# Seven small moves of work and waits in a two-layer trunk kernel: empty steps, earlier transposes, new homes, and 16 writes on another queue

## The chip, the core and the metric

The kernel runs on one core of a Trainium2 chip. The metric is the device time of one execution in microseconds. A core has five engines with queues of their own, each of which runs its instructions in order: TensorE (PE, matrix products into PSUM), VectorE (DVE), ScalarE (ACT), GpSimd (POOL) and SyncE (SP, which here issues nearly all DMAs). [...] PE's clock is granted by a throttle; 1.00 is full speed.

## The reference

One sequence of 1024 tokens, width 1024, float32, two layers. The core of it, with norms left out:

```python
for layer in range(2):
    hn = rms_norm(h, ...)
    if layer == 0:                     # "even": gated MLP + gated delta rule
        a_uv, b_qkv, b_z, b_beta, b_a = split(hn @ w_in_e)
        a_out = gmlp_spatial_gate(gelu(a_uv), ...)      # 128-token chunks, 4 groups
        b_out = gated_deltanet(b_qkv, b_z, ...)         # 64-token chunks, 4 heads, unit lower-triangular solves
        h = h + concat([a_out, b_out]) @ w_out_e
    else:                              # "odd": differential attention, 8 heads x 2 maps, alibi, causal
        o = diff_attention(hn @ w_qkv_o, ...)
        h = h + o @ w_out_o
    h = h + square(relu(rms_norm(h) @ w_mlp1[layer])) @ w_mlp2[layer]      # width 4096
    h = h + (p[layer] @ w_ple_proj[layer]) * sigmoid(rms_norm(h) @ w_ple_gate[layer])
```

## The kernel before, in words

**Tiles.** The residual h lies in DRAM (`h_dram`) as eight feature tiles of 128 features by 1024 tokens; in SBUF it is held as two halves of 512 tokens (`h` or `hf` = 0, 1), so a tile is 128x512. Nearly every product of full width is done with three float32r matmuls: each operand is split into a rounded part `hi` (an ACT cast, line 221) and a remainder `lo` (a DVE subtraction, line 222), and `mm3` (line 204) multiplies hi·hi, hi·lo and lo·hi. A call of `mm3` is called a unit below. Weights come through a ring of eight `raw` buffers (`RB = 8`), `TB = 4` scratch tiles are shared through `tmp()`, and PSUM has two buffers for each of the tags mm, tr, aux and sc.

**The order.** The program is traced in Python and then ordered by a planner, which issues, on each engine, what its own time model finds ready, by priority (the order of writing; `high_priority` raises it). `Ordered.behind` adds an order of issue without a semaphore. `pe.floor` puts the next PE instructions behind a given one.

**Layer 0, `even_mix` (line 1281).** The projections are a generator `fill`; `pump(n)` advances it. The delta rule's serial chain is cut into steps, and `chunk` (nested in `even_mix`) issues, for each entry of its list `parts`, the steps that the letters name ("s" the state's recurrence, "i" the inverse, "p" the preparation) and then a share of units of `fill`. First `solve` (line 1670) solves the 32x32 diagonal blocks on DVE and stores them to `solved`; then `inverse(c)` (line 1714) loads them back (`inv<-solved`), transposes them on DVE (line 1728), and merges blocks to 128 by products `py`, `pz` on PE with copies between them; the last copy (line 1764) completes `xt`, which `step(c)` reads in its product `pvn`. For the first chunk the call is

```python
chunk(none, invs[0], f0, FILLC, ("p", "i", "i", "i", "i", "ip"), bound=True)
```

with `FILLC = 48` units over six entries; `bound=True` sets a floor, so that a step comes behind the units already issued. The eight chunks that follow hide their chain under the other projections, and `mix_out` (line 1229) closes the stage.

**Layer 1, `attention` (line 893).** A loop over 64 blocks (8 heads x 8 query blocks of 128) calls `pump()` four times per block. Each call advances the q/k/v projections by the table `MARKS` (call number, units done), and, past call `TAIL`, one step of `tails()`: `put_halves` (line 1113) reads stored attention outputs back from `o_dram` into a ring of four, `put_o` (line 1103) transposes one on PE (tag tr) and splits it on ACT and DVE into the buffers that held the normed h; `mix_part` (line 1205) then multiplies the first 6 (half 0) or 5 (half 1) heads by `w_out`, adds the residual row tile from DRAM (line 1225) and stores it. After the loop `mix_out` does the remaining heads, 2 for half 0 and 3 for half 1; between its steps the two functions in `close` are called: the last block's value product, and `put_o(7, 1)`, which needs that block's output scaled by POOL (line 1099). At its end, for half 0, it computes the rms of h (matmuls with ones, a POOL power at line 258, matmuls that spread the rows, an ACT copy to `rb`, line 265) and splits the normed h for the MLP (lines 1268 to 1273).

**MLP and PLE.** `mlp` (line 275) is a seven-product (Strassen-Winograd) scheme. In layer 1 its output tiles are also stored token by token: `turn` (line 516) transposes 32x32 blocks on DVE and issues four DMAs of 64 KB to `by_token`. `ple_out` (line 634) is again a seven-product scheme; `raw` (line 651) loads weight blocks into the `raw` ring, `rows` (line 700) reads residual rows from `by_token`, `close` gates and stores the output.

Of the kernel before, what the change touches and what calls it, by code (L numbers as in the profile page):

```python
# [11 lines left out]
F32 = mybir.dt.float32  # L12
# [6 lines left out]
P = 128  # L19
# [12 lines left out]
KA = (6, 5)  # L32
MARKS = ((64, 50), (192, 144), (223, 168))
TAIL = 220
FILLA, FILLB, FILLC = 36, 60, 48
# [79 lines left out]
class Trunk:  # L115
# [132 lines left out]
    def rms(self, half, sqs, ms=None, rows=True):  # L248

        nc = self.nc  # L250
        if ms is None:
            pt = self.aux_ps()
            for t in range(4):
                self.pe.matmul(pt[:, t : t + 1], lhsT=sqs[:, t * P : (t + 1) * P], rhs=self.ones[:, 0:1], start=True, stop=True)
            ms = self.sp.tile([P, 4], F32, tag="ms", name=self.nm("ms"))
            nc.vector.tensor_scalar(ms, pt[:, 0:4], 1.0 / D, EPS, ALU.mult, ALU.add)  # L256
        r = self.sp.tile([P, 4], F32, tag=f"r{half}", name=self.nm("r"))
        nc.gpsimd.tensor_tensor(r, ms, self.mhalf[:, 0:4], ALU.pow)  # L258
        rb = None
        if rows:  # L260
            pb = self.aux_ps()
            for t in range(4):
                self.pe.matmul(pb[:, t * P : (t + 1) * P], lhsT=r[:, t : t + 1].to_broadcast([P, P]), rhs=self.ident, start=True, stop=True)
            rb = self.sp.tile([P, HT], F32, tag=f"rb{half}", name=self.nm("rb"), bufs=1)
            nc.scalar.copy(rb, pb)
        return r, rb

    def mlp(self, x, x_tags, gain, w1, w2, gain_next, h_dram, p, last):
# [239 lines left out]

        def turn(m, h):

            t = self.tmp()
            nc.vector.transpose(t, acc[m][h])
            for i in range(4):  # L520
                f0 = (m % 4) * P + 32 * i
                nc.sync.dma_start(by_token[h][m // 4].rearrange("(a c) f -> c a f", c=32)[:, :, f0 : f0 + 32], t[32 * i : 32 * i + 32].rearrange("c (a r) -> c a r", r=32))

# [110 lines left out]
    def ple_out(self, pT, acc, by_token, gain, wg, wpj, out):  # L634
# [258 lines left out]
    def attention(self, w_qkv, w_out, gain_next, h_dram):  # L893
# [3 lines left out]
        hs, r = list(self.hs), list(self.r)  # L897
        self.mixed = [[None] * KT, [None] * KT]

        al = self.slot("B", [P, S], F32, "al")  # L900
# [212 lines left out]
        def put_halves():  # L1113
# [42 lines left out]
        def tails():  # L1156
            puts = put_halves()
            for hf in range(2):
                while state[1] < 160 + 8 * hf:
# [9 lines left out]
        for g in range(8 * NB + 2):  # L1169
# [35 lines left out]
    def mix_part(self, h, n, w_out, h_dram):  # L1205
# [3 lines left out]
        def load(m):  # L1209
            if m < KT:  # L1210
                res = self.tmp()
                nc.sync.dma_start(res, h_dram[m, :, cols])
                return res

        ahead = load(0)
        for m in range(KT):
            if m % 2 == 0:
                w = self.weight(w_out[0 : n * P, m * P : (m + 2) * P], n, 256, nc.gpsimd)
            res, ahead = ahead, load(m + 1)
# [5 lines left out]
            nc.vector.tensor_tensor(res, res, ps, ALU.add)  # L1225
            nc.sync.dma_start(h_dram[m, :, cols], res)


    def mix_out(self, h, acc, w_out, h_dram, gain_next, k0=0, late=0):

# [5 lines left out]
        for m in range(KT):  # L1236
# [5 lines left out]
            ps = begun.pop() if begun else self.mm_ps()  # L1242
            if late and m == 0:
                begun.append(self.mm_ps())
                for q, k in itertools.product(range(2), range(late, n)):
                    self.mm3((ps, begun[0])[q], w.at(k, slice(q * P, (q + 1) * P)), self.mixed[h][k0 + k], k == late, False)
                    yield
            for i in range(n - late if late and m < 2 else 0, n):
                k = (i + late) % n
# [4 lines left out]
                self.pe.floor = None  # L1254
                if i < n - 1:
                    yield
# [5 lines left out]
        if h == 0:  # L1262
            self.rb[0] = self.rms(0, self.sqs[0])[1]
            self.rb_mark = self.pe.mark
            lows = []
            for m in range(KT):
                a = acc(m)
                inst = nc.vector.scalar_tensor_tensor(a, a, gain_next[:, m : m + 1], self.rb[0], ALU.mult, ALU.mult)
                if m > 1:
                    self.pe.behind(inst, lows[m - 2])  # L1270
                hi, lo = self.hs_new[0][m] = self.hs_parts(0, m)
                nc.scalar.copy(hi, a)  # L1272
                lows.append(nc.vector.tensor_tensor(lo, a, f32(hi), ALU.subtract).ins.name)  # L1273
        yield
# [6 lines left out]
    def even_mix(self, first, rows_of_rest, rest_of_x, w_in, ws, bs, conv, a_log, dt_bias, v_gain, o_gain, masks, w_out, gain_next, h_dram):  # L1281
# [432 lines left out]
        def inverse(c):  # L1714
# [47 lines left out]
            for h in range(G):  # L1762
                self.pe.matmul(pz[:, h], lhsT=x64[:, h], rhs=yt[:, h], start=True, stop=True)
            (nc.vector.tensor_copy if c < NC - 1 else nc.scalar.copy)(xt[0:64, :, 64:P], pz)
            ch[c] = xt
# [56 lines left out]
        def mixing():  # L1822
# [9 lines left out]
            side = second_gates()  # L1832
            yield from beside(self.mix_out(0, acc, w_out, h_dram, gain_next, late=G), side, 4, 8)
            for _ in side:
# [111 lines left out]
def trunk(tc, x, p, ln_mix_e, w_in_e, gmlp_v_gain, gmlp_ws, gmlp_bs, gdn_conv, gdn_a_log, gdn_dt_bias, gdn_out_gain,  # L1946
          w_out_e, ln_mix_o, w_qkv_o, attn_q_gain, attn_k_gain, diff_lambda, attn_sub_gain, w_out_o, ln_mlp, w_mlp1,
          w_mlp2, ln_ple, w_ple_gate, w_ple_proj, masks, out):
    with ExitStack() as ctx:
# [54 lines left out]
        for layer in range(2):  # L2004
# [68 lines left out]
```

## Time and profile before

| | us |
|---|---|
| median of 3 runs | 2499.24 |
| lowest, highest | 2496.97, 2501.38 |
| the profiled execution's own time | 2502.64 |
| its span (first to last instruction) | 2500.9 |
| PE busy | 2471.4 (99%) |
| DVE / ACT / POOL busy | 1866.2 / 1289.2 / 303.9 |

The mean granted clock of PE is 0.996. A row of waits reads "engine, tile, line that waited <- what ended the wait: total, times, longest". A row of a timeline reads "start, duration, engine, line, operation, out<-in, shape, count", and in brackets the idle time before it with what ended it. `SPq` rows are DMA issues in SP's queue. In rows of stretches, each engine's busy time is followed by its count of instructions, then come the granted clock, DMA share and GB/s.

### The profile page before, as it was taken

Reading aid. Unit: us, or ns where it says so; the run is one execution under the profiler, and the core shown is the slowest. Engines: PE = TensorE matmul, PEld = TensorE weight load, DVE = VectorE, ACT = ScalarE, POOL = GpSimd, SP = SyncE. Lnnn points to the kernel's source line nnn. Section 1 sums busy time; section 2 is a strip of 40 time slices with the busy share of each in tenths; the row PEclk is TensorE's granted clock in tenths of the full one; section 3 lists DMA queues with packets and bytes.
Section 4 is the critical chain, followed back from the end, with each engine's and each line's share of the span. In section 5 each row is a group of like instructions: output and inputs, shape, how many; then the busy total and the mean of one; then the engine's idle time right before and its main releaser. Section 6 shows DMA issues by size and latency. Waiting matters only on the chain.

```text
span 2500.9 us, 39804 instructions
## 1 busy us (share of the span) xinstructions
PE 2471.4 (99%) x13567; PEld 2108.1 (84%) x13567; DVE 1866.2 (75%) x3642; ACT 1289.2 (52%) x2585; POOL 303.9 (12%) x272
## 2 busy tenths in 40 slices
PE   9999999999999999999999999999999999999999
PEld 7898897888888887888899999987788888887877
DVE  7787776597667879566568888886886677788677
ACT  6543443465455435454366766664655455445443
POOL 0211231000000000000244443431000000000000
PEclk9999999999999999999999999999999999999999
DMA  8384645457556856553347776799375558657773
GB/s 253 114 248 115 171 142 178 140 161 246 169 182 224 264 180 191 187 173 111 119 100 167 163 173 153 174 252 287 125 235 191 173 187 283 213 180 202 237 215 110
DMA packets 567924, 461.96 MB, mean 185 GB/s; under 512 B 256676, under 2 KB 429736, under 8 KB 567720
## 3 DMA queue, kind: packets, MB, share of 16 engines
q1 hardware_dynamic: 533912, 455.21, 60.3%
q10 hardware_dynamic: 33808, 4.20, 1.1%
q8 instruction: 107, 1.75, 0.3%
q14 instruction: 97, 0.79, 0.1%
HBM read 322.95 MB, written 136.33 MB: 184 GB/s over the span
## 4 chain that ended last, share of the span: by engine, by line
PE 89%; DVE 4%; DMA 4%; issue 1%; ACT 1%; SPq 1%; POOL 0%; ACTq 0%; DVEq 0%; POOLq 0%
PE mm L76 78%; PE po L76 3%; PE qk L76 2%; PE aux L76 2%; PE tr L79 1%; DMA raw<-in_w_ple_gate_dram 1%; DMA raw<-in_w_mlp_dram 1%; DVE w L222 1%; DMA spill<-early 0%; DMA a_dram<-lg 0%; DMA guv<-uv_dram 0%; DVE acc L282 0%; DMA aT<-a_dram 0%; DVE g L222 0%; PE pvn L76 0%
## 5 line engine op out<-in xcount | busy, mean ns | idle before, releaser
L76 PE MATMUL mm<-g,w 128*128 128x512 f32 x2592 | 604.0, 395 | 1.5 <-DVE g L222 1.1
L221 ACT CAST w<-raw 128x512 fp32r<-128x512 f32 x598 | 365.0, 616 | 449.6 <-PE mm L76 364.7
L76 PEld LDWEIGHTS mm<-g,w 128*128 128x128 f32 x2592 | 486.7, 188 | 116.5 <-DVE g L222 2.0
L76 PE MATMUL mm<-hi,w 128*128 128x512 f32 x1728 | 555.2, 398 | 0.3 <-ACT hi L1272 0.3
L76 PE MATMUL mm<-w,hi 128*128 128x256 f32 (+2 forms) x2528 | 504.9, 295 | 0.8 <-ACT t L1500 0.6
L222 DVE TENSOR_TENSOR w<-raw,w 128x512 fp32r<-128x512 f32 (+1 forms) x510 | 349.6, 692 | 167.9 <-ACT w L221 160.4
L76 PEld LDWEIGHTS mm<-w,hi 128*128 128x128 f32 x2528 | 402.8, 189 | 16.0 <-ACT t L1500 0.8
L76 PEld LDWEIGHTS mm<-hi,w 128*128 128x128 f32 x1728 | 325.4, 189 | 74.3 <-ACT hi L1272 0.7
L76 PE MATMUL mm<-w,lo 128*128 128x256 f32 (+2 forms) x1264 | 368.5, 292 | 0.0
L76 PE MATMUL mm<-lo,w 128*128 128x512 f32 x864 | 341.6, 395 | 1.0 <-DVE lo L1273 1.0
L76 PE MATMUL mm<-t,w 128*128 128x512 f32 x1152 | 270.7, 394 | 1.2 <-ACT w L221 1.2
L76 PEld LDWEIGHTS mm<-t,w 128*128 128x128 f32 x1152 | 216.5, 188 | 52.2 <-ACT w L221 1.6
L76 PEld LDWEIGHTS mm<-w,lo 128*128 128x128 f32 x1264 | 238.2, 189 | 5.8
L76 PEld LDWEIGHTS mm<-lo,w 128*128 128x128 f32 x864 | 163.4, 189 | 38.0 <-DVE lo L1273 1.4
L222 DVE TENSOR_TENSOR g<-graw,g 128x512 fp32r<-128x512 f32 x216 | 147.5, 687 | 11.2 <-DMA gd<-g 6.8
L221 ACT CAST g<-graw 128x512 fp32r<-128x512 f32 x216 | 132.6, 617 | 43.9 <-DMA graw<-gd 16.4
L1048 ACT ACTIVATE lg<-lg,nm 128x128 f32<-128x128 f32 (+7 forms) x128 | 99.2, 776 | 77.0 <-DVE nm L1045 76.2
L258 POOL TENSOR_TENSOR r<-ms,mhalf 128x4 f32<-128x4 f32 x12 | 13.2, 1103 | 1006.7 <-DVE ms L256 981.2
L222 POOL TENSOR_TENSOR w<-raw,w 128x512 fp32r<-128x512 f32 (+1 forms) x88 | 115.4, 1330 | 142.3 <-ACT w L221 85.0
L348 ACT ACTIVATE g<-g 128x512 f32<-128x512 f32 x96 | 60.5, 631 | 119.3 <-DVE g L282 112.4
L1045 DVE CUSTOM_DVE_ANT_0 lg<-qk,al 128x512 f32<-128x512 f32 (+3 forms) x128 | 74.7, 587 | 27.2 <-PE qk L76 22.0
L76 PE MATMUL mm<-ohi,w 128*128 128x512 f32 x256 | 87.1, 405 | 0.7 <-DVE t L1225 0.7
(332 smaller groups left out, 3522.0 us busy)
## 6 DMA issues: line engine op xcount, KB each, us to landing
raw<-in_w_mlp_dram SPq DMA_DIRECT2D x352, 256.0 KB, 3.4
graw<-gd SPq DMA_DIRECT2D x224, 256.0 KB, 2.8
gd<-g SPq DMA_DIRECT2D x192, 256.0 KB, 3.0
raw<-in_w_ple_gate_dram SPq DMA_DIRECT2D x76, 256.0 KB, 3.6
acc<-h_dram SPq DMA_DIRECT2D x64, 256.0 KB, 4.3
keep<-in_w_mlp_dram SPq DMA_DIRECT2D x64, 256.0 KB, 4.5
raw<-in_w_in_e_dram SPq DMA_DIRECT2D x60, 256.0 KB, 3.7
h_dram<-acc SPq DMA_DIRECT2D x48, 256.0 KB, 2.7
```

The source lines that it names most:

```text
L76: self._next(self.engine.matmul(*a, **k))
L79: self._next(self.engine.transpose(*a, **k))
L221: self.nc.scalar.copy(hi, src)
L222: (lo_engine or self.nc.vector).tensor_tensor(lo, src, f32(hi), ALU.subtract)
L258: nc.gpsimd.tensor_tensor(r, ms, self.mhalf[:, 0:4], ALU.pow)
L348: nc.scalar.activation(g, src, AF.Relu)
L1045: nc.vector.tensor_tensor_reduce(out=lg[:, k0:k1], in0=ps[:, : k1 - k0], in1=al[:, u0 + k0 : u0 + k1], scale=-1.0, scalar=3.0e38 if c == 0 ...
L1048: nc.scalar.activation(lg[:, :n], lg[:, :n], AF.Exp, bias=nm[:, r, nch - 1 : nch], scale=-1.0, accum_out=me.sums[:, b, r : r + 1])
```

## The change

- **First inverse.** Three empty entries stand between "p" and the first "i"; the 48 units are shared over nine entries and not six.
- **Last copy of an inverse.** For chunks 4 to 6 ACT does it and not DVE (chunk 7 had ACT already).
- **Tail of the attention.** `TAIL` 220 becomes 205 and the last mark moves from call 223 to 227; `put_halves` issues its first four loads when `tails` starts; `begin` of the last head comes one block earlier.
- **`mix_part`.** Residual rows get homes of their own (slots c0, c1 and sqs0 in turn, and no longer a `tmp`), are loaded two tiles ahead, and a tile is closed (added, stored) after the second unit of the next tile.
- **`mix_out` in layer 1.** `put_o(7, 1)` is called after step 16 of half 0 and not after step 12; half 1 begins with heads 5 and 6 of its first two tiles; the rms sums of half 0 are issued at tile 2 of half 1 and its rows at tile 4, where before both came at the end of half 0, held ahead of tile 6.
- **`turn`.** The 16 writes of the last four tiles are issued from GpSimd's queue and no longer from SP's.
- **`ple_out`.** The first four residual rows go to tiles lo10 to lo13 and no longer to four of the eight `raw` buffers.

```diff
-MARKS = ((64, 50), (192, 144), (223, 168))
-TAIL = 220
+MARKS = ((64, 50), (192, 144), (227, 168))
+TAIL = 205
...
-        def turn(m, h):
+        def turn(m, h, queue=nc.sync):
...
-                turn(q, 1)
+                turn(q, 1, nc.gpsimd)
...
-        rows(0, 0, [self.raw(1, HT)[:, 0] for _ in R])
+        rows(0, 0, [self.hp.tile([P, HT], F32, tag=f"lo1{q}", name=self.nm("rows")) for q in R])
...
             for n in range(4):
                 load(n)
+            yield
...
-                if b == 6 + (hd == 6) and hd < 7:
+                if b == 6 and hd < 7:
                     begin(hd + 1)
...
+                i = next(self.res_home)
+                res = self.slot(f"c{i}", [P, HT], F32, "res") if i < 2 else self.sp.tile([P, HT], F32, tag="sqs0", name=self.nm("res"), bufs=1)
...
+        def close():
+            m, ps = open_.pop(0)
+            res = ahead.pop(0)
+            self.pe.behind(nc.vector.tensor_tensor(res, res, ps, ALU.add), self.pe.mark)
+            nc.sync.dma_start(h_dram[m, :, cols], res)
+            load(m + 2)
...
+                if m and k == 1:
+                    close()
...
-                if h == 1 and k0 and (m, i) == (6, 0):
-
-                    self.pe.floor = self.rb_mark
+            if h == 1 and k0 and m in (2, 4):
+                self.pe.floor = self.pe.mark
+                self.later.pop(0)()
+                self.pe.floor = None
...
+            def sums():
+                self.r[0] = self.rms(0, sqs, rows=False)[0]
+
+            def rows():
+                self.rb[0] = self.rows(0, self.r[0])
+                lows = []
+                for m in range(KT):
...
+            self.later = [sums, rows]
+            if not k0:
+                sums()
+                rows()
...
-            (nc.vector.tensor_copy if c < NC - 1 else nc.scalar.copy)(xt[0:64, :, 64:P], pz)
+            (nc.vector.tensor_copy if c < G else nc.scalar.copy)(xt[0:64, :, 64:P], pz)
...
-        chunk(none, invs[0], f0, FILLC, ("p", "i", "i", "i", "i", "ip"), bound=True)
+        chunk(none, invs[0], f0, FILLC, ("p", "", "", "", "i", "i", "i", "i", "ip"), bound=True)
...
-                    if n + 1 in (4 * (KT - KA[0]), 6 * (KT - KA[0])):
+                    if n + 1 in (4 * (KT - KA[0]), 8 * (KT - KA[0])):
                         close.pop(0)()
-            for _ in T.mix_out(1, lambda m: acc_of(m, 1), (w_out_e, w_out_o)[layer][0], h_dram, gain[3 * layer + 1], KA[1] * layer):
+            for _ in T.mix_out(1, lambda m: acc_of(m, 1), (w_out_e, w_out_o)[layer][0], h_dram, gain[3 * layer + 1], KA[1] * layer, first=(0, 1) if layer else ()):
```

More of the change, by code (lines that the diff above doesn't have):

```diff
@@ L258, in rms, with rows @@
         nc.gpsimd.tensor_tensor(r, ms, self.mhalf[:, 0:4], ALU.pow)
[L259 to L266, printed above, removed]
+        return r, self.rows(half, r) if rows else None
+    def rows(self, half, r):
+        pb = self.aux_ps()
+        for t in range(4):
+            self.pe.matmul(pb[:, t * P : (t + 1) * P], lhsT=r[:, t : t + 1].to_broadcast([P, P]), rhs=self.ident, start=True, stop=True)
+        rb = self.sp.tile([P, HT], F32, tag=f"rb{half}", name=self.nm("rb"), bufs=1)
+        self.nc.scalar.copy(rb, pb)
+        return rb
     def mlp(self, x, x_tags, gain, w1, w2, gain_next, h_dram, p, last):
@@ L1157, in tails @@
             puts = put_halves()
+            next(puts)
             for hf in range(2):
@@ L1222, in mix_part, with mix_out @@
                 self.mm3(ps, w.at(k, slice((m % 2) * P, (m % 2 + 1) * P)), self.mixed[h][k], k == 0, k == n - 1)
+                if m and k == 1:
+                    close()
                 if k % 2:
                     yield
-            nc.vector.tensor_tensor(res, res, ps, ALU.add)
-            nc.sync.dma_start(h_dram[m, :, cols], res)
-    def mix_out(self, h, acc, w_out, h_dram, gain_next, k0=0, late=0):
+            open_.append((m, ps))
+        close()
+    def mix_out(self, h, acc, w_out, h_dram, gain_next, k0=0, first=()):
         nc = self.nc
@@ L1832, in mixing @@
             side = second_gates()
-            yield from beside(self.mix_out(0, acc, w_out, h_dram, gain_next, late=G), side, 4, 8)
+            yield from beside(self.mix_out(0, acc, w_out, h_dram, gain_next, first=range(G, KT)), side, 4, 8)
             for _ in side:
```

42 lines of the change are left out of this document (20 added, 22 removed).

## The prediction

> **What bounds the kernel now.** First the page, for the engine that is always busy, then what PE waits for.
>
> ```profile
> span 2500.9 us, 39804 instructions
> PE 2471.4 (99%) x13567; PEld 2108.1 (84%) x13567; DVE 1866.2 (75%) x3642; ACT 1289.2 (52%) x2585; POOL 303.9 (12%) x272
> ```
>
> PE sets the time. No edit takes a matmul away, so all that can be won is the 2500.9 - 2471.4 = 29.5 us in which PE is idle, and whatever the idle time costs afterwards. The view of PE's waits lists it nearly whole:
>
> ```profile
> engine line waited for: us in total, times, longest us
> PE py L76 <- issue: 4.4, 1, 4.4
> PE aux L76 <- DVE ms L256: 3.3, 1, 3.3
> PE pvn L76 <- DVE xt L1764: 2.5, 1, 2.5
> PE tr L79 <- POOL o L1099: 2.1, 1, 2.1
> PE tr L79 <- DVE ss L938: 1.6, 1, 1.6
> ...
> PE mm L76 <- DVE lo L1273: 1.0, 1, 1.0
> ...
> PE mm L76 <- DVE t L1225: 0.7, 1, 0.7
> ```
>
> Single waits, each at one place; that makes the question seven small questions. The four longest have an aftermath, which the view of stretches shows where the granted clock (after POOL's figure) falls:
>
> ```profile
> core 0: us, PE busy (x) PEld busy (x) DVE busy (x) ACT busy (x) POOL busy (x), PEclk, DMA share, GB/s
> 207.32:212.11 4.79, 4.79 (x26) 3.86 (x27) 2.21 (x6) 0.53 (x3) 0.00 (x0) 0.50 0.35 55
> 382.78:386.19 3.41, 3.41 (x14) 2.92 (x13) 1.18 (x5) 0.41 (x1) 0.33 (x1) 0.50 0.88 266
> 1737.87:1741.28 3.41, 3.41 (x11) 2.83 (x10) 1.49 (x3) 1.78 (x3) 0.00 (x0) 0.50 0.20 77
> 2417.12:2420.53 3.41, 3.41 (x10) 2.63 (x9) 2.53 (x5) 0.74 (x2) 0.46 (x1) 0.50 0.68 199
> ```
>
> PE is busy there, but at half speed, so half of each stretch is lost: 2.4 us after the first wait, 1.7 us after each of the other three. A wait of 2.1 us costs 3.8 us. [...]
>
> **The change part by part.**
>
> *A. Empty entries before the first inverse.* The timelines of SP, DVE and PE in turn:
>
> ```profile
> 198.91 0.34 SPq L1685 DMA_DIRECT2D solved<-work  x1
> 202.56 0.33 SPq L1723 DMA_DIRECT2D inv<-solved  x1
> 206.91 0.31 DVE L1728 STREAM_TRANSPOSE inv<-inv 128x128 f32<-128x128 f32 x1 [0.63 <-DMA inv<-solved]
> 201.16 0.63 PE L76 MATMUL mm<-hi,w 128*128 128x512 f32 x2
> 201.86 0.63 PE L76 MATMUL mm<-hi,w 128*128 128x512 f32 x2
> 207.32 0.64 PE L76 MATMUL py<-inv,am 32*32 32x32 f32 x16 [4.38 <-issue]
> ```
>
> The product py stands in PE's order after two entries of 8 units, but its operand makes a round trip through DRAM (store at 198.91, load from 202.56, transpose at 206.91). With nine entries (5, 5, 6, 5, 5, 6, 5, 5, 6) py comes after 26 units and not 16. A unit takes 201.86 - 201.16 = 0.70 us, so PE has 10 x 0.70 = 7.0 us more to do before it, against 4.38 us of waiting: 2.6 us of cover is left. Saved: 4.38 + 2.4 = 6.8 us (ends 0 and 6.8). Late next: the inverse's steps now lie 5 to 6 units (3.5 to 4.2 us) apart and not 5.6; what lies between two of them on DVE and ACT is a few copies, and the LAG of three slots gives 10 us of room. No instruction is added. I book 1 us for a step that comes late.
>
> *B. The last copy on ACT for chunks 4 to 6.* Timeline of DVE, then ACT:
>
> ```profile
> 378.25 2.18 DVE L1544 SCALAR_TENSOR_TENSOR guv<-guv,rv,vg 128x128 f32<-128x128 f32 x8
> 380.34 0.69 DVE L222 TENSOR_TENSOR w<-raw,w 128x512 fp32r<-128x512 f32 x1
> 380.94 0.41 DVE L1764 COPY xt<-pz 64x256 f32<-64x256 f32 x1
> 378.98 0.59 ACT L1580 CAST ahi<-pab 128x512 fp32r<-128x512 f32 x1 [1.26 <-PE pab L79]
> ```
>
> Chunk 6's copy queues on DVE behind nine instructions of other work, while ACT had been idle 1.26 us before 378.98. On ACT it can run at about 378, before PE reaches pvn. Saved: 2.5 + 1.7 = 4.2 us (0 to 4.2). For chunks 4 and 5, where PE did not wait, ACT takes on 0.4 us; it is 52% busy, so nothing is booked.
>
> *C. `put_o(7, 1)` four units later.*
>
> ```profile
> 1736.58 1.04 POOL L1099 TENSOR_TENSOR o<-o,of 128x512 f32<-128x512 f32 x1
> 1737.67 0.97 PE L79 MATMUL tr<-ident,o 128*128 128x128 f32 x4 [2.07 <-POOL o L1099]
> ```
>
> PE stood from 1735.60 until POOL was done. Four units are 2.8 us, over 2.07. The transposes' split, needed by head 7's products, is then covered by the four units of heads 5 and 6 that half 1 now begins with. No DMA moves. Saved: 2.07 + 1.7 = 3.8 us (0 to 3.8).
>
> *D. Sums at tile 2, rows at tile 4.* In the groups of the stretch 1753.8 to 1770 and on the page:
>
> ```profile
> L1268 DVE SCALAR_TENSOR_TENSOR acc<-acc,cols,rb 128x512 f32<-128x512 f32 x8 | 5.9, 747 | 0.8 <-ACT rb L265 0.8
> ...
> L258 POOL TENSOR_TENSOR r<-ms,mhalf 128x4 f32<-128x4 f32 x12 | 13.2, 1103 | 1006.7 <-DVE ms L256 981.2
> ```
>
> Before, the rows are held only ahead of tile 6 of 8; now they start at tile 4, two tiles of three units earlier, 4.2 us, against the 1.0 us that the MLP's first `lo` is late. Between sums and rows lie the same 4.2 us for a POOL power of 1.1 us. Saved 1.0 us (bounds -1 to 1.0: a row product that comes too early holds PE's queue).
>
> *E. `ple_out`: four `raw` buffers freed, 16 writes off SP.* Timelines of SP and DVE, then the view of `by_token`:
>
> ```profile
> 2408.04 2.56 SPq L522 DMA_DIRECT2D by_token<-t  x4
> 2410.70 7.34 SPq L653 DMA_DIRECT2D raw<-in_w_ple_gate_dram  x6
> 2415.73 0.69 DVE L643 TENSOR_TENSOR raw<-raw,raw 128x512 f32<-128x512 f32 x1 [2.92 <-DMA raw<-in_w_ple_gate_dram]
> 2416.34 0.15 DVE L256 TENSOR_SCALAR ms<-aux 128x4 f32<-128x4 f32 x1
> 2416.57 1.01 POOL L258 TENSOR_TENSOR r<-ms,mhalf 128x4 f32<-128x4 f32 x1 [67.58 <-DVE ms L256]
> 2418.20 0.17 DVE L734 TENSOR_SCALAR rh<-r 128x4 f32<-128x4 f32 x1
> ...
> L522 SPq DMA_DIRECT2D by_token<-t x16: 326/488/1062, 2395.2 to 2410.1; - x16
> ```
>
> The 3.3 us at ms is not ms's own: ms stands in DVE's queue behind a subtraction that waits 2.92 us for a weight block. Those loads wait in SP's queue behind the writes (16 x 0.49 = 7.8 us of issue) and for a free `raw` buffer, four of which hold residual rows. Both causes go. Saved: 3.3 + 1.7 = 5.0 us (0 to 5.0). What the GpSimd queue asks for its writes, no row shows; POOL issues no DMA in this program. Let w be its time for one. Lower bound: SP's 0.49 us. Upper bound: a write moves 64 KB in runs of 128 B, 512 of them on each side; if one run costs as much as one column of the 512-column POOL product (1.04 us, part C), two sides make 2.1 us, and with the fixed part of a small POOL instruction (1.01 us above) 3.1 us. I take 1.5 us, the small instruction and a quarter of the rest, since writing out a run's address is less than reading and multiplying. The power at 2416.57 now stands behind all 16 writes, the first of which is ready at 2395.2; free of cost up to w = (2416.57 - 2395.2)/16 = 1.34 us. At 1.5 it is 16 x 0.16 = 2.6 us late, and DVE, in whose queue rh (line 734) waits for it, with everything behind. I book 2 us, as PE still has products in hand.
>
> *F. Tail of the attention.* Residual rows with homes of their own, two tiles ahead, end the 0.7 us at `t L1225`; no instruction is added, the 16 loads and 16 stores stay on SP. Transposing stored outputs earlier, the reads already issued, goes for the 1.6 us at `ss L938`, where the transposes wait for a tr buffer that DVE has not emptied; six outputs bring 12 ACT and DVE passes into the last projections, whose DVE is full too. Booked: 0.7 + 0.8 = 1.5 us (0.0 to 2.3). The head begun a block earlier: nothing, its transposes lie under the same projections.
>
> *Sum.* 6.8 + 4.2 + 3.8 + 1.0 + 5.0 + 1.5 = 22.3 us, less 1 (A) and 2 (E): about 19.5. The traced execution's own time was 2502.64 us, so it would be 2483.1; it lies 3.4 us above the median of the runs, 2499.24, and against that I predict **2480 us**. Under 0.2% (5 us) this measurement can hardly tell from no change.
>
> **The rivals.**
>
> *R1, slower: POOL as a queue.* Place: the power of the second half and rh behind the 16 writes. Each us of w above 1.34 costs 16 us. At the upper bound, 3.1 us, the delay is 28 us against 22.3 - 1 = 21.3 won: 2499 + 28 - 21 = 2506 us. It decides from w = 1.34 + 21.3/16 = 2.7 us. For it: the writes are many short runs, and scratch tiles (four in all) stay taken until a write lands. Against it: 512 runs at POOL's pace per column give only 1.04 us a side. [...] Chance 0.15.
>
> *R2, part of it: waits move.* The planner orders anew on every engine; a step of A or a tr buffer of F comes late, or w is near 2 us (a delay of 10.6). Half of 19.5 is lost: 2490 us. For it: in the whole first stage DVE and ACT queues decide by tenths who is late, as part B shows. Chance 0.25.
>
> *R3, no change.* All the waits are replaced by others of their size: 2499 us. Against it: PE's idle time lies at a few places, and each edit adds cover larger than the wait it meets (A 7.0 over 4.38, C 2.8 over 2.07). Chance 0.08.
>
> **How the numbers follow.** The forecast, 2480 with its own range 2471 to 2486, has 0.52; R2 (2486 to 2494) 0.25; R3 (to 2504) 0.08; R1 0.15. Faster by over 0.2% (under 2494.2): 0.52 + 0.25 = 0.77; same 0.08; slower 0.15. The low end is the sum without deductions and with all of F, 2499.2 - 23.1 = 2476, less the 5 us of other small waits and of the runs' spread: 2471, rounded to 2470. The high end takes in R2 and most of R3: 2500. Outside are R1 and a remnant of R3.
>
> **What would show it.** Right: py without a wait and 0.50 nowhere near 207; a copy at line 1764 on ACT before pvn and no wait at pvn; no wait at `tr <- POOL o`; PE idle well under 15 us in all. Wrong: POOL's queue still in writes when the power is due, DVE idle at line 734, PE waiting on aux or sc tiles after it; a new wait at pz or at pvn of chunk 0; clock rows of 0.50 at places that now have none.

## The result: faster, by well under half of the forecast

The changed kernel takes 2493.55 us (median of 20 runs, 2491.23 to 2498.89); the kernel before, beside it, 2501.63 us (20 runs). The ratio is 0.9970, with a 95% interval of 0.9963 to 0.9977: 7.5 us faster (5.8 to 9.3). The forecast was 19.5 us. The sign was right, the size was not: 2493.55 us lies inside the whole range given (2470 to 2500), but outside the forecast's own range (2471 to 2486).

The page of the changed kernel, and the view of what PE waits for (us in total, times, longest):

```profile
span 2493.6 us, 39815 instructions
...
PE 2466.9 (99%) x13567; PEld 2105.9 (84%) x13567; DVE 1863.5 (75%) x3639; ACT 1288.5 (52%) x2588; POOL 314.5 (13%) x288
```

```profile
engine line waited for: us in total, times, longest us
PE mm L76 <- DVE res L1220: 3.3, 2, 2.3
PE po L76 <- DMA aT<-a_dram: 2.6, 4, 0.8
PE tr L79 <- POOL o L1094: 2.5, 1, 2.5
PE aux L79 <- DMA x<-in_x_dram: 2.4, 1, 2.4
PE mm L76 <- ACT t L1520: 1.8, 1, 1.8
PE qk L76 <- DVE ql L1006: 1.6, 1, 1.6
...
PE py L76 <- issue: 0.8, 1, 0.8
PE pst L76 <- ACT qkv L1807: 0.7, 1, 0.7
```

PE still stands 2493.6 - 2466.9 = 26.7 us, against 29.5 before. What left: py fell from 4.4 to 0.8, pvn from 2.5 to nothing (0.7 at `pst` in its place), `ms` from 3.3 to nothing: 8.7 us. What came: 3.3 us at `res` (line 1220, the closing of a partial projection; 0.7 before, under the name `t`), 2.6 us at `aT` (0.3 before), 2.5 us at the last turned output, where C should have taken away 2.1. Most of it lies in the tail of the attention, from 1625 to 1742 us; about 1.1 us of the wait at `aT` come earlier. (Two more waits are longer than before, 2.4 us at `x`, right at the start, and 1.8 us at `t`, line 1520, at 156 us. PE's order of instructions is the same as before up to 204 us, so the change did not move them; over all profiled executions below they lie between 1.2 and 2.4 and between 0 and 2.6 us.)

The half-clock stretches moved the same way. Stretches of 3.41 us of the changed kernel (the columns are those of the prediction's view):

```profile
core 0: us, PE busy (x) PEld busy (x) DVE busy (x) ACT busy (x) POOL busy (x), PEclk, DMA share, GB/s
1629.19:1632.60 3.41, 1.76 (x13) 1.57 (x14) 2.94 (x10) 2.46 (x7) 1.64 (x1) 1.00 0.93 289
1632.60:1636.01 3.41, 3.41 (x16) 3.22 (x15) 3.05 (x11) 2.61 (x11) 0.00 (x0) 0.50 0.56 92
1724.76:1728.17 3.41, 1.09 (x6) 0.56 (x5) 1.94 (x4) 1.66 (x3) 0.00 (x0) 1.00 0.23 70
1728.17:1731.58 3.41, 3.41 (x10) 2.63 (x9) 3.31 (x6) 2.34 (x5) 0.00 (x0) 0.50 0.81 227
1738.41:1741.82 3.41, 0.94 (x7) 0.72 (x7) 1.02 (x2) 0.07 (x1) 2.43 (x3) 1.00 1.07 396
1741.82:1745.24 3.42, 3.42 (x10) 2.65 (x9) 0.75 (x1) 0.61 (x1) 0.00 (x0) 0.50 0.23 81
```

The stretches at 207, 382 and 2417 us are gone; in the tail there are three where there was one. So the question is what the tail did with its share.

### The profile page after: what moved, and what is told of

Same layout as the page of the kernel before. It is cut to its first block, busy times and chain, and to the rows that moved or that the text cites. A ratio compares the mean times of both kernels' runs of the same rounds, so it can differ in the third digit from the quotient of the medians.

```text
span 2493.6 us, 39815 instructions
## 1 busy us (share of the span) xinstructions
PE 2466.9 (99%) x13567; PEld 2105.9 (84%) x13567; DVE 1863.5 (75%) x3639; ACT 1288.5 (52%) x2588; POOL 314.5 (13%) x288
## 4 chain that ended last, share of the span: by engine, by line
PE 92%; DMA 3%; DVE 3%; issue 1%; ACT 1%; SPq 0%; POOL 0%; DVEq 0%; ACTq 0%; POOLq 0%
PE mm L76 81%; PE po L76 3%; PE qk L76 2%; PE aux L76 2%; DMA a_dram<-lg 1%; PE tr L79 1%; DMA aT<-a_dram 0%; DMA h_dram<-res 0%; PE pks L76 0%; DMA res<-h_dram 0%; PE pz L76 0%; PE py L76 0%; PE pkq L76 0%; PE pgm L76 0%; PE aux L79 0%
```

## The experiments

Every kernel below is compared with the kernel before on the same chip. A difference of two ratios means something only where their intervals part.

| run | what it is | median us | ratio (95%) |
|---|---|---|---|
| the change | all parts | 2493.6 | 0.9970 (0.9963 to 0.9977) |
| abe_only | before + A, B, E | 2488.8 | 0.9944 (0.9930 to 0.9959) |
| cdf_only | before + C, D, F | 2510.2 | 1.0035 (1.0023 to 1.0047) |
| home_sqs1 | change, third home sqs1 | 2499.9 | 0.9988 (0.9979 to 0.9996) |
| writes_sp | change, writes back on SP | 2497.4 | 0.9980 (0.9971 to 0.9989) |
| homes4 | change, four homes | 2501.2 | 0.9997 (0.9989 to 1.0006) |
| part_old | change, `mix_part` as before | 2489.8 | 0.9949 (0.9937 to 0.9962) |
| turns_old | change, turns as before | 2500.5 | 0.9998 (0.9989 to 1.0007) |
| chain_early | change, last chain first | 2492.7 | 0.9964 (0.9951 to 0.9976) |
| close_now | change, closings as before | 2498.7 | 0.9980 (0.9970 to 0.9989) |
| rows_scratch | change, rows in scratch | 2488.9 | 0.9945 (0.9933 to 0.9957) |
| old_part_chain | part_old + chain_early | 2488.7 | 0.9943 (0.9931 to 0.9955) |
| lead2 | change, homes4 + close_now, early loads | 2502.0 | 0.9993 (0.9983 to 1.0002) |
| loads_pool | change, row loads by GpSimd | 2497.4 | 0.9983 (0.9973 to 0.9992) |
| scratch_chain | rows_scratch + chain_early | 2488.6 | 0.9949 (0.9935 to 0.9963) |
| scratch_turns_old | rows_scratch + turns_old | 2485.2 | 0.9938 (0.9923 to 0.9953) |
| a_only | before + A | 2497.0 | 0.9985 (0.9975 to 0.9995) |
| abe_homes | abe_only + homes | 2502.3 | 0.9998 (0.9989 to 1.0007) |
| scratch_turns_chain | rows_scratch + turns_old + chain_early | 2485.1 | 0.9926 (0.9914 to 0.9939) |

### Two halves, and the first suspect

**abe_only** and **cdf_only** split the change: the edits in the first stage and in `ple_out`, and those in and around the attention's tail.

> The kernel before with parts A (empty entries), B (last inverse copy on ACT) and E (homes of the rows, 16 writes by GpSimd) alone; the attention's tail is as before. By the traces of before and after, PE's waits there fell by 4.4 - 0.8, 2.5 - 0.7 and 3.3 us, and 2.4, 1.7 and 1.7 us of half clock went with them: 14.5 us. Theory H (the loss lies in the tail): ratio about 0.9942, 2487 us. Rival P (these parts gave only what the whole change gave, since the ends of waits in the first stage turn up elsewhere): ratio 0.997, 2494 us.

> The kernel before with parts C, D and F alone, the edits in and around the attention's tail. Theory H: it is slower than before, by what the tail lost in the trace of after: the new wait at res 2.3 us and its half clock 1.7 us, the longer wait of 2.5 in place of 2.1 us at the turned output, up to 2 us at the transposed blocks, less the 1 us of part D: 4 to 6 us, ratio 1.0016 to 1.0024. Rival P: the tail neither wins nor loses, ratio 1.000.

A, B and E give 14.0 us (10.3 to 17.5); booked were 6.8 + 4.2 + 5.0 less 3, 13.0 us. C, D and F, booked at 3.8 + 1.0 + 1.5 = 6.3 us of gain, cost 8.8 us (5.8 to 11.8). The halves add up to 5.2 us, beside 7.5 for the whole. The error of the prediction lies in the tail, and it is one of sign.

The first suspect came from ACT's timeline in the changed kernel:

```profile
start us, us, engine line op out<-in xcount [idle before <-releaser]
...
1725.07 0.63 ACT L237 ACTIVATE sqs<-acc 128x512 f32<-128x512 f32 x1 [5.33 <-DMA h_dram<-res]
```

The first square of `mix_out` writes sqs0, the third home, and waits 5.33 us until the last residual row has been stored out of it. **home_sqs1** gives that row another tile:

```diff
-... self.sp.tile([P, HT], F32, tag="sqs0", name=self.nm("res"), bufs=1)
+... self.sp.tile([P, HT], F32, tag="sqs1", name=self.nm("res"), bufs=1)
```

> The changed kernel with one edit: the third home of the residual rows is the tile sqs1, which nothing needs for another 20 us, in place of sqs0, which the first square of the output projection's half 0 needs at once. Theory H (the home): ACT's first square waits 5.3 us for the store of the last residual row out of sqs0, casts and closings queue behind it, PE waits 2.3 us at mm for res and then runs 3.4 us at clock 0.50. Without it the 5.3 us and the 2.3 us are gone, with the 1.7 us of the half clock: 4.0 us less than the changed kernel, ratio to before about 0.995; if the bunched closings are also what keeps the turning of the last output late (2.5 us and 1.7 us), up to 8 us less, ratio about 0.994. Rival L (the loads): DVE waits 14.5 us in all for residual rows still on their way from DRAM, and the home plays no part: the 2.3 us stay, ratio 0.997.

It got slower: 0.9988. The square no longer waits for a store (it stands 5.63 us for DVE instead), and PE's longest wait at `res` grew from 2.3 to 7.0 us, with DVE 16.3 us without work until a row landed. The conflict at sqs0 is real and is not what the tail pays for.

### Which part of F

**homes4** has four homes; **part_old** puts back the whole old `mix_part` (rows in `tmp()`, closing at the tile's end); **turns_old** puts back `TAIL`, `MARKS`, `begin` and the start of `put_halves`.

```diff
-        self.res_home = itertools.cycle(range(3))
+        self.res_home = itertools.cycle(range(4))
-... tag="sqs0" ...
+... tag=("sqs1", "rb1")[i - 2] ...
```

> The changed kernel with four homes for the residual rows in turn (c0, c1, sqs1, rb1) in place of three (c0, c1, sqs0): a load never waits for the store of the tile just closed, and the output projection's first square waits for none. Theory H+L (the homes: sqs0 holds ACT's first square, and with three homes each load stands in SP's queue behind the landing of a store one tile back, which is also why the run with sqs1 was worse, with DVE 16.3 us without work until a row came): the waits of PE at mm for res go (0.9, 2.3 us and 1.7 us of half clock), 4 to 5 us less than the changed kernel, ratio 0.995; up to 8 us if the turned output profits. Rival M (the earlier turning of stored outputs crowds DVE, ACT and SP among the last blocks): 0.997.

> The changed kernel with the partial projections' rows and closings as before: rows in the scratch ring, loaded one tile ahead, closed at the end of the tile. Everything else as changed. Theory H+L (the homes and closings are what made the tail slower): it gets back the loss of the tail, ratio about 0.994. Rival M (the earlier turns): it stays at 0.997 or gets worse, since the rows are again only one tile ahead.

> The changed kernel with the turning of stored outputs, the marks of the fill and the begin of head 7 as before; homes and closings as changed. Rival M (the six early turns are what made the tail slower): the waits at aT (2.6 us) and at ql and qh (2.1 us, half clock 1.7 us) go, ratio about 0.994. Theory H+L: those waits change place only, the wait at res of 2.3 us with its half clock stays, ratio 0.997.

part_old gets 5.3 us back, so the new `mix_part` is to blame. More homes are no cure (0.9997). And turns_old went the other way from what the rival M expected: without the earlier turns the new `mix_part` is 7 us worse. The early turns are no cause of the loss; where the homes are, they soften it.

The new `mix_part` differs from the old in two things, the place of the rows and the place of the closing. **close_now** and **rows_scratch** undo one each:

```diff
# close_now
-                if m and k == 1:
-                    close()
             open_.append((m, ps))
-        close()
+            close()
# rows_scratch
-                i = next(self.res_home)
-                res = self.slot(f"c{i}", ...) if i < 2 else self.sp.tile(..., tag="sqs0", ...)
+                res = self.tmp()
```

> The changed kernel with one edit: a partial projection's tile is closed right behind its last product, as before, and not behind the second product of the next tile; the three homes and all else as changed. Theory K (the later closing: the sum tile of each product comes free two units, 1.4 us, later, so PE waits for it as soon as a residual row is late, and store and next load follow later too): the 5.3 us that the run with the old closings and rows won come back, ratio 0.995. Rival H (the homes): it stays at 0.997.

> The changed kernel with one edit: the residual rows lie in the scratch ring again, and not in c0, c1 and sqs0; closings behind the second product of the next tile as changed. Rival H (with three homes each load waits in SP's queue for the landing of a store, 7.4 us in all against 1.0 us before, and sqs0 holds ACT's first square 5.3 us): these go, ratio 0.995. Theory K (the later closing): 0.997; worse if the scratch ring of four, of which three are then taken, holds the squares.

Theory K, the later closing, falls: with the closing back at its place and the homes kept it is 0.9980, no better than the change. With the rows back in the scratch ring and the late closing kept it is 0.9945. The homes are it.

**abe_homes** asks the same from the other side: the kernel with A, B and E, its tail as before, and only the tiles of the residual rows changed.

```diff
-                res = self.tmp()
+                i = next(self.res_home)
+                res = self.slot(f"c{i}", ...) if i < 2 else self.sp.tile(..., tag="sqs0", ...)
```

> The kernel before with parts A, B and E (0.9944 by themselves) and one thing more: the residual rows of the partial projections lie in c0, c1 and sqs0 in turn, not in the scratch ring; loads one tile ahead, closings at the end of the tile, turns and everything else of the tail as before. Theory H (the homes by themselves are what costs): 0.997 to 0.999, with waits of SP for stores of residual rows of 7 us or more. Rival: the homes cost only together with the later closings and earlier turns: 0.9944 to 0.995.

0.9998 against 0.9944: 13.5 us for a choice of three tiles, with no instruction added, and more than theory H expected. The views of what SP and DVE wait for, both over the stretch 1600 to 1755 us; first abe_only (SP, then DVE), then abe_homes, then the changed kernel:

```profile
SPq L1212 <- DMA h_dram<-t: 0.3, 1, 0.3
```

```profile
DVE t L1225 <- DMA t<-h_dram: 5.0, 2, 4.7
```

```profile
SPq L1214 <- DMA h_dram<-res: 16.1, 6, 5.0
```

```profile
DVE res L1227 <- DMA res<-h_dram: 16.1, 3, 10.2
```

```profile
SPq L1210 <- DMA h_dram<-res: 11.5, 6, 2.9
```

```profile
DVE res L1220 <- DMA res<-h_dram: 14.5, 3, 10.6
```

Lines 1212, 1214 and 1210 are the same load of a residual row. It stands at the head of SP's queue until the store of an earlier row out of the same tile has landed: 0.3 us in all from the scratch ring, 16.1 us with homes. SP issues in order (in abe_homes, below, the load `ol` is issued 5.6 us later, behind two such loads), so the loads of transposed blocks (`aT`), accumulators and weights behind it wait too; and the row comes late, so that DVE stands 16.1 us and not 5.0. All profiled executions fall into two groups by it: the wait of that load for a row's store is 0.2 to 1.6 us in the nine with scratch, and 7.1 to 16.1 us in nine of the ten with homes that SP fills (21.1 us in the tenth, close_now). In the ring of four, a row's tile is also handed to the squares of the same stage, so the next load often takes a tile whose last user was no store; a home has in this stage nothing in it but rows. Within the homes, however, the size of the wait does not order the ratios: 7.1 us in lead2 (0.9993), 11.5 us in the change (0.9970), 15.0 us in writes_sp (0.9980). Nor is DVE's wait for rows a price by itself: it is 11.8 us in scratch_chain, which has its rows in scratch and runs at 0.9949.

Where PE pays can be read for the pair above. In its profiled execution PE stands 25.6 us in abe_only and 32.8 us in abe_homes, and 5.1 us are lost in one long stretch at half clock in the tail of abe_homes, where abe_only lost 1.7 us: 7.2 + 3.4 = 10.6 us, beside 10.3 us between the two spans. The largest single piece shows the way through SP's queue. First abe_only, where the load `ol` of a stored output is issued in time for its transpose:

```profile
1680.57 0.44 SPq L1121 DMA_DIRECT2D ol<-o_dram  x1
1684.99 0.63 PE L79 MATMUL tr<-ident,ol 128*128 128x128 f32 x4 [0.18 <-DVE nm L1045]
```

Then the same load in abe_homes, the row load ahead of it, and what followed:

```profile
1683.45 0.33 SPq L1214 DMA_DIRECT2D res<-h_dram  x1
1686.19 0.64 SPq L1122 DMA_DIRECT2D ol<-o_dram  x1
1690.61 1.09 PE L79 MATMUL tr<-ident,ol 128*128 128x128 f32 x4 [3.38 <-DMA ol<-o_dram]
```

```profile
1689.20:1692.61 3.41, 2.00 (x7) 1.84 (x8) 0.15 (x1) 0.88 (x2) 0.00 (x0) 0.50 0.98 246
```

The execution runs about 1.9 us later by then, but `ol` is issued 5.6 us later: two row loads that come behind it in abe_only stand ahead of it here, and waited 3.7 us for stores. PE waits 3.4 us at `ol` and then runs 10.24 us at half clock. turns_old has the same pattern, 3.0 us at `ol` and 10.24 us at half clock; the change, which turns the stored outputs earlier, has no wait at `ol`. That fits the 7 us by which the early turns soften the loss, but is not the whole of it: close_now has the early turns and still waits 3.9 us there.

Two runs tried to loosen the knot and keep the homes. **lead2** loads each row at the start of the tile two ahead, into four homes, ahead of the closings; **loads_pool** lets GpSimd issue the loads.

```diff
# lead2 (beside homes4 and close_now)
+            load(m + 2)              # at the start of tile m
-            load(m + 2)              # in close()
# loads_pool
-                nc.sync.dma_start(res, h_dram[m, :, cols])
+                nc.gpsimd.dma_start(res, h_dram[m, :, cols])
```

> The changed kernel with closings right behind the tile's last product, four homes (c0, c1, sqs1, rb1), and each residual row loaded at the start of the tile two ahead, not behind a closing: the load no longer follows the store of the tile before in SP's queue. Theory L (the rows are late because load, closing and store make a loop): DVE's waits for rows (14.5 us) and PE's for res go, better than the run with the old closings, ratio 0.993 to 0.994. Rival Q (the 16 DMA queues are full from 1695 to 1715 us, share 0.96 to 1.06, so that a load issued earlier only takes from another): no better than 0.995.

> The changed kernel with the 16 loads of residual rows issued by GpSimd in place of SP; homes and closings as changed. Theory S (in SP's queue a load waits 11.5 us in all for stores of residual rows to land, and the loads of transposed blocks, accumulators and weights behind it wait with it): SP no longer waits there and the tail gets back to 0.995. Rival W (the rows come late wherever they are issued, and the closing waits): 0.997 to 0.998, DVE's wait for rows still 10 us or more. Third case: GpSimd's weight splits now stand behind the loads, slower than 0.998.

Neither did. In lead2 the load waits 7.1 us at SP's head and the `aT` loads 7.7 us more for stores of rows. In loads_pool the wait leaves line 1210 of SP and comes back at the loads of `acc` (line 1250), which read rows from h_dram that those stores write; SP first, then GpSimd:

```profile
SPq L1250 <- DMA h_dram<-res: 12.2, 7, 4.4
```

```profile
POOL res L1210 <- DMA h_dram<-res: 10.7, 3, 9.1
```

So the block at SP's head is not by itself the whole price: moved to another queue, the wait for the stores was paid again elsewhere. That the homes cost 6 us in the change and 13.5 us beside the old tail is shown; that it comes through waits for row stores is argued from the traces: it fits the two groups and the wait at `ol`, and not the order within the homes. Which of the two ways, queue or late row, carries more of it in the change itself stays open, and so does why a fourth home doesn't break the chain.

### The last turned output (C)

In the prediction the last output is late because POOL is; four more units were to cover it. DVE's timeline of the changed kernel, then POOL's:

```profile
1733.63 0.69 DVE L241 TENSOR_TENSOR sqs<-sqs,t 128x512 f32<-128x512 f32 x1
1734.23 0.16 DVE L1088 TENSOR_TENSOR osq<-osq,c 128x4 f32<-128x4 f32 x1
1734.30 0.68 DVE L1267 TENSOR_TENSOR acc<-acc,mm 128x512 f32<-128x512 f32 x1
1734.90 0.69 DVE L241 TENSOR_TENSOR sqs<-sqs,t 128x512 f32<-128x512 f32 x1
1735.50 0.16 DVE L1089 TENSOR_TENSOR osq<-osq,c 128x4 f32<-128x4 f32 x1
1735.58 0.69 DVE L222 TENSOR_TENSOR w<-raw,w 128x512 fp32r<-128x512 f32 x1
1736.18 0.68 DVE L1267 TENSOR_TENSOR acc<-acc,mm 128x512 f32<-128x512 f32 x1
1736.78 0.69 DVE L241 TENSOR_TENSOR sqs<-sqs,t 128x512 f32<-128x512 f32 x1
1737.38 0.17 DVE L1090 TENSOR_SCALAR osq<-osq 128x4 f32<-128x4 f32 x1
```

```profile
1737.69 1.92 POOL L1092 TENSOR_TENSOR of<-osq,mhalf 128x4 f32<-128x4 f32 x1 [34.05 <-DVE osq L1090]
...
1739.96 1.04 POOL L1094 TENSOR_TENSOR o<-o,of 128x512 f32<-128x512 f32 x1
```

DVE has no gap here. The three small steps that POOL waits for (`osq`) stand between closings of 0.6 us a pass, and each tile of two units (1.4 us of PE) brings an `acc` and a `sqs` pass, 1.2 us, most often with a weight split of 0.6. Four units more for PE are two closings more for DVE ahead of the chain: the cover grows and so does what it covers. **chain_early** puts the last block's chain first:

```diff
+                last = hd == 7 and b == NB - 1
+                early = self.tc.high_priority(EARLY) if last else contextlib.nullcontext()
+                early.__enter__()
                 nc.scalar.copy(o[b // 4][:, b % 4, :], po)
-                sq = self.tmp(P)
+                sq = self.sp.tile([P, HT], F32, tag="rb1", ...)[:, 0:P] if last else self.tmp(P)
...
                 nc.gpsimd.tensor_tensor(o[hf], o[hf], ...)
+                if last:
+                    early.__exit__(None, None, None)
```

> The changed kernel; the chain from the last block's output to the scaled o (ACT copy and square, three small DVE products, three POOL products) goes ahead of the closings of the output projection in the order of ACT and DVE, and its square has a tile of its own. Theory D (in part C the four units bring two closings of 1.3 us each on DVE ahead of the chain, so DVE, not the distance in units, sets when o is ready): o is ready 3 us or more earlier, the wait of 2.5 us at tr for o goes, and 1.7 us of half clock: 4.2 us less than the changed kernel, ratio 0.9953. Rival: the last block's product itself is late, or PE then waits for the closings instead: 0.997.

> The run with the old closings and rows of the partial projections, and with the last block's chain ahead of the closings on ACT and DVE. The 3.2 us wait at tr for the last o, which stands in that run's trace, goes: if nothing takes its place, 3 to 5 us less than that run, ratio 0.993 to 0.9937; if DVE's closings are late in its place, as the run with the early chain alone hints (three new waits of 0.8 to 1.1 us), no difference, 0.995.

> The changed kernel with the residual rows in the scratch ring and the last block's chain ahead of the closings. By theory D the wait of 2.5 us at tr for the last o goes, and nothing else: 2.5 us less than with the rows alone, and up to 1.7 us of half clock in part of the runs, ratio 0.993 to 0.9935. If two or three waits of about 1 us in the rows of the MLP take its place, as in the runs with the chain before, no difference: 0.9945.

Theory D is right on the wait: the 2.5 us at `tr` are gone in all profiled executions with the early chain. But it won nothing that can be told: 0.9964 against 0.9970, 0.9943 against 0.9949, 0.9949 against 0.9945, all within their intervals. In its place PE waits 1.1 us at `hi` and 1.1 us at `lo` of the MLP's first tiles, the wait that D was to end.

### What the earlier turns are worth, A alone, the writes, and the best version

> The changed kernel with the residual rows in the scratch ring and the turning of stored outputs, marks and begin of head 7 as before. If the early turns are worth what the prediction booked (0.8 us, at most 1.6): 0.9948 to 0.995. If they are worth what the two runs with homes differ by (7 us): 0.997. If they only crowd the last blocks: below 0.9945.

> The changed kernel with the rows in the scratch ring, the turns of stored outputs as before, and the last block's chain ahead of the closings: what is left of the run with old turns (0.9938) less its wait of 2.9 us at tr for the last o. If nothing takes its place 0.9927; if waits of about 1 us in the rows of the MLP do, 0.9938 as without it.

With the rows in scratch, the old turns (0.9938) and the new (0.9945) can't be told apart: so the 7 us between turns_old and the change were a cure for what the homes had brought. scratch_turns_chain, the change with rows in scratch, old turns and the early chain, is the fastest kernel here, 0.9926, 18.5 us (15.3 to 21.5) less than before; its interval parts from that of the change, not from that of scratch_turns_old. Its page and PE's longest waits:

```profile
span 2481.7 us, 39833 instructions
...
PE 2461.3 (99%) x13567; PEld 2102.0 (85%) x13567; DVE 1864.0 (75%) x3639; ACT 1290.6 (52%) x2588; POOL 313.3 (13%) x288
```

```profile
PE mm L76 <- ACT t L1522: 1.8, 1, 1.8
PE aux L79 <- DMA x<-in_x_dram: 1.6, 1, 1.6
PE tr L79 <- DVE ss L933: 1.6, 1, 1.6
```

No wait is over 1.8 us any more.

**a_only** is the kernel before with the three empty entries alone (the diff of part A).

> The kernel before with the empty entries ahead of the first inverse alone (part A). By the traces, 3.6 us of the wait at py and 2.4 us of half clock go: 6 us, ratio 0.9976; the prediction booked 5.8. If a later step pays it back: 0.999 or more.

3.8 us (1.3 to 6.3), with 5.8 booked: smaller at the point, and the interval holds the booking. In its profile py waits 0.9 us where it waited 4.4, as expected.

**writes_sp** returns the 16 writes to SP (`turn(q, 1)`), the rows keep their new tiles.

> The changed kernel with the 16 last writes of by_token back on SP; the rows keep their new homes. If the queue matters as the prediction had it, the weight loads stand again behind up to 7.8 us of issue and some of the 3.3 us wait and its 1.7 us of half clock come back: up to 5 us more than the changed kernel, ratio 0.998 to 0.999. If the freed buffers alone did it: no difference, 0.997. If the later landing of the GpSimd writes (4.5 against 2.4 us) costs anything, up to 2 us less.

0.9980 against 0.9970 is 2.5 us, but the intervals overlap (0.9971 to 0.9977), so the ratios show no difference. In the trace PE's wait at `ms`, 2.5 to 3.3 us in the three kernels without E and gone with the change, is back in part:

```profile
PE aux L76 <- DVE ms L256: 1.6, 1, 1.6
```

So the queue takes away a part of that wait and the freed buffers the rest; what the queue alone is worth in time is not shown.

## Why the prediction was right and wrong, step by step

- **A: right on the wait, its cover taken twice too large.** py 4.4 to 0.8 us, no stretch at 0.50 after it; alone it gave 3.8 us. The prediction said "PE has 10 x 0.70 = 7.0 us more to do before it", with 2.6 us to spare. In the traces 1221 matmuls stand ahead of py before and 1236 in the change. The 15 more are five units, 3.5 us, less than the 4.38 us of the wait; the rest is the wait that was left:

```profile
208.61 0.44 PE L76 MATMUL py<-inv,am 32*32 32x32 f32 x16 [0.77 <-issue]
```

  Why the order gave five units and not ten is not shown.
- **B: right**, 2.5 to 0.7 us: the rest is a new wait at `pst`, for ACT's copy of the product pvn, for which nothing was booked.
- **E: right, and its deduction wrong.** The wait at `ms` is gone. No run has B or E alone; A, B and E less A alone leave 14.0 - 3.8 = 10.2 us for the two, where 4.2 + 5.0 less 2 were booked. The price of a GpSimd write was taken as w = 1.5 us between 0.49 and 3.1. The view of the `by_token` writes in the changed kernel has the 16 (ns: least, median, most):

```profile
L516 POOL DMA_DIRECT2D by_token<-t x16: 648/651/855, 2393.0 to 2406.5; - x16
```

  w is 0.65 us, near the lower bound and under the 1.34 from which it costs anything. The 2 us taken off were not needed, and rival R1 (slower from w = 2.7) falls. The issue of a write took longer on GpSimd than SP's 0.49 us, by a third and not by a factor. That writing out a run's address is less than reading and multiplying was an estimate; no run shows what GpSimd does in the 0.65 us.
- **C: wrong in the step "Four units are 2.8 us, over 2.07".** The units were counted as cover without the work that they bring for DVE, in whose queue the late chain stands. The wait was 2.5 us, where it had been 2.1. With the chain early it is gone, and still no time is won that can be told, so the 3.8 us booked for C were not found.
- **D: right on the mechanism**; the wait at `lo` is gone in the change, and comes back as 1.1 and 1.1 us where the last output is early. It was 1 us before and can't be seen in a ratio.
- **F: wrong, and this is the step that failed the forecast.** It said: "Residual rows with homes of their own, two tiles ahead, end the 0.7 us at `t L1225`; no instruction is added, the 16 loads and 16 stores stay on SP", booked at 0.7 us with a range that ended at 0. The instructions are indeed the same. What changed is what each of them waits for: a tile used by nothing but rows can't be loaded before its last row has been stored (11.5 us of such waits at SP's head in the change, 0.3 us from the scratch ring in abe_only). The homes cost 6 us in the change (0.9970 against 0.9945) and 13.5 us with the old tail (0.9998 against 0.9944). "Two tiles ahead" was also less than it sounded: the load for tile m + 2 is written behind the store of tile m, as before. Both come two units later, which close_now and rows_scratch show to be no cause, and the row lies elsewhere. No row of before shows a load into a tile of its own, so the range should have gone below nothing there, by what stands behind such a load in SP's queue. The homes make up about 6.3 of the 12.0 us between forecast and result, since the change with its rows in scratch is 13.8 us faster. The other 5.7 us are nearly the 5.6 booked for C, D and the turns, which together won nothing that can be told: rows_scratch has them (0.9945), abe_only does not (0.9944).
- **F, the turns:** booked 0.8 us, worth nothing that can be told (0.9945 against 0.9938 with them undone). The wait at `ss L938`, 1.6 us, gave way to one of 1.6 us at `ql`.
- **The rivals.** The size is near that of R2 (half lost because waits move), and the causes that R2 named, a late step of A, a late tr buffer, w near 2 us, are none of them the one. Of the prediction's own signs, those at py and pvn came out nearly as said; a wait at `tr <- POOL o` stayed, PE stood 26.7 us where "well under 15 us" was said, and rows at 0.50 stand at new places. The 18.5 us of scratch_turns_chain come near the forecast by another way, with the early chain and without the early turns, and are no proof of its sum.

## What to carry to other kernels

A buffer of its own is no freedom by itself: ask what its last user was, and if that was a store, expect the next load into it to wait at the head of its queue until the store has landed, as the row loads did here (11.5 us in the change, 16.1 us in abe_homes), with all that stands behind it. When a late step is given more work to hide behind, count that work on every engine, above all the one in whose queue the late step stands, and count the units in the order that is really issued, not in the list from which it is made. And when an edit is booked at "no instruction added", look at what each instruction will wait for before writing a zero as the end of its range.

## What was not expected of the hardware

**What a wait cost in clock depended on where it fell.** The prediction charged 1.7 us for each wait over 2 us. In part_old PE waits 3.2 us at the last output, more than any wait of the changed kernel, and no half clock follows:

```profile
1727.95:1731.36 3.41, 1.70 (x7) 1.05 (x6) 3.25 (x6) 0.63 (x1) 1.40 (x1) 1.00 1.07 402
1731.36:1734.77 3.41, 1.92 (x11) 1.66 (x12) 0.51 (x1) 0.69 (x1) 1.28 (x3) 1.00 0.61 219
1734.77:1738.18 3.41, 3.41 (x21) 2.92 (x19) 1.69 (x5) 1.33 (x3) 0.60 (x1) 1.00 0.18 62
```

These stretches, like those of the changed kernel above, are laid on the grid on which the clock changed: within one execution all its changes lie whole multiples of 3.41 us apart (in the changed kernel half clock begins at 1632.60, 1728.17 and 1741.82 us, 28 and 4 times 3.41 us apart). The wait is split by the grid into 1.71 and 1.49 us, and the clock stays at 1.00. In the changed kernel at 1629.19 a stretch with 3.41 - 1.76 = 1.65 us of idle is followed by one at 0.50, in the kernel before at 1628.64 one with 3.41 - 1.86 = 1.55 us is not. Over the 20 profiled executions, cut on that grid and counting stretches at full clock, each of the 41 with 1.90 us of idle or more is followed by half clock, none of the 21 with 1.50 to 1.62 us is, and 8 of 25 between; one exception, with 1.30 us, stands against it. So here the same wait cost 1.7 us or nothing by its place on the grid, and 1.65 us of idle in a stretch could be enough for the drop; what sets it is not shown.

**A write by GpSimd landed later than one by SP**, 4.5 us (median of 16) against 2.4 us (of 48) for the same 64 KB in the changed kernel. PE has no wait in that stretch (2380 to 2440 us); ACT waits 0.5 us for one such write.
